# RMSNorm and matmul on one core: loads of x two pairs of tiles earlier, squares up to two pairs earlier, inverse roots in the pair after their roots

## The chip, the core and the metric

The kernel runs on one core of a Trainium2 chip. The core has five engines, each with its own instruction stream: TensorE (matmuls and transposes; PE in the profile, PEld its weight loads), VectorE (DVE), ScalarE (ACT), GpSimd (POOL) and SyncE (SP). An engine works through its stream in order and stops in front of an instruction whose semaphores are not there yet. Transfers between the chip's main memory and the on-chip memory (SBUF) are issued by an engine and then carried out by 16 DMA engines; here SyncE and ScalarE issue them, each on a queue of its own. Matmul results stand in PSUM, from which VectorE or ScalarE copies them.

The metric is the device time of one execution in microseconds; lower is better.

## The reference

Each of the 16 x 1024 rows of `x` (512 numbers, float32) is divided by its root mean square, multiplied by `gamma`, and multiplied by a 512 x 768 matrix.

```python
def reference(x, gamma, weight, eps):
    rms = np.sqrt(np.mean(x ** 2, axis=-1, keepdims=True) + eps)
    x_norm = x / rms * gamma
    return np.matmul(x_norm, weight).astype(np.float32)
```

`x` is 33.6 MB, the output 50.3 MB.

## The kernel before

**Tiles and pairs.** The 16,384 rows make NT = 128 tiles of 128 rows, worked on in NP = 64 pairs; the main loop (L414) runs over pairs j, with tiles 2j and 2j + 1. `gamma` is folded into the weights once at the start (`weights`, L374). The division by the root mean square is done last, on the matmul's result, since it is one number per row.

**One tile's way.** A load brings eight tiles at once into `xt` (two buffers of 16 tiles, so 32 tiles are on chip; L154). GpSimd casts them to bf16 (`cast`, L185, into `xb`; `cast_quad`, L266, into `xq`). TensorE transposes the `xb` tiles into PSUM (`transpose_word`, L235) and VectorE copies them out into `xT` (`evac`, L244). The last four tiles of each 16 ("quads") go another way: VectorE transposes blocks of 32 x 32 from `xq` to `xTq` (`move`, L279, three of sixteen in each pair), and TensorE has no transposes for them. TensorE then makes eight matmuls for each tile into one of three accumulators in PSUM (`matmuls`, L315; `product`, L307). The result is scaled by the inverse root of the row and written to `ot` (`finish_tile`, L326): the even tile of a pair by ScalarE (L288), the odd one by VectorE (L290). `ot` has three buffers of eight tiles; when the eighth is written, SyncE stores the buffer (`store`, L297, issue at L302). A tile can be written into a buffer only after the store of three groups ago has landed.

**The norms.** ScalarE squares each tile with a running sum (`square`, L194: two instructions, L205), which goes to `ssq`. For a group of four pairs it then takes the roots at once (`root`, L208, instruction L210), and VectorE inverts them (L212) into `rstd`, which both scales read. `NORM_GROUPS` (L221) lists the groups: pairs 5 and 6, then 7 to 10, 11 to 14 and so on, and the last five. `norm_turns` (L223) says which pairs are squared in turn j: from j = 7 on pair j + 4. Before that the first pairs are squared one or two at a time.

**Loads.** `load_until` (L181) issues loads in order up to a tile. The first 32 tiles are loaded at the start on SyncE's queue, with the weights; the twelve loads from tile 32 on go on ScalarE's queue (`load`, L174), so each stands in ScalarE's stream among squares and scales. L429 issues the load of tiles 32 to 39 at j = START = 4 and the others at every j > 4 with (j + LEAD) divisible by 4, up to tile 2(j + LEAD) + 8. With LEAD = 14 that is j = 6, 10, 14, ...: tiles 2(j + 14) onwards, fourteen pairs ahead. Such a load overwrites the tiles 32 before, and waits for their squares and casts.

**What sets the order.** The code lists operations in one sequence (`Order`, L21), with what each reads and writes; each engine's stream is its share of the sequence, and `emit` (L39) adds the waits. So the place of a call in the loop is its place in its engine's stream. In turn j come, in this order: casts, moves (L424), norms (L425 to L428), loads (L429), then the pair's matmuls, with the transposes of pair j + 2 between them (`feeder`, L334), and the two scales.

Of the kernel before, what the change touches and what calls it, by code (L numbers as in the profile page):

```python
# [100 lines left out]
def kernel(  # L101
# [12 lines left out]
    def run(engine, issue, reads=(), writes=()):  # L114
        order.add(1, engine, issue, reads, writes)
# [6 lines left out]
    NT = N // P  # L122
    NP = NT // 2
    XG, OG = 16, 8
    FIRST, START, LEAD = 2 * XG, 4, 14

    def stretches(group, parts):
        first, size, i = {}, {}, 0
# [45 lines left out]
    def load(i):  # L174
        dst, to = x_of(i, x_size[i])
        queue = SP if i < FIRST else ACT
        order.transfer(queue, lambda: queue.dma_start(out=dst, in_=rows(x, i, x_size[i])), writes=to)
# [3 lines left out]
    def load_until(i):  # L181
        while starts and starts[0] < i:
            load(starts.pop(0))

    def cast(i, n=1):  # L185
        src, of = x_of(i, n)
        s = i // 8 % 2
        run(POOL, lambda: POOL.tensor_copy(out=xb[s][:, i % 8:i % 8 + n, :], in_=src), of, cells("xb", s, i % 8, n))  # L188
# [5 lines left out]
    def square(i):  # L194
        src, of = x_of(i)
        n = squares[0]
        squares[0] += 1
        if n < 4:
            to, dst = [("jk", n % 2)], jk[n % 2]
        else:  # L200
            n = (n - 4) % SPARE
            to, dst = [("spare", n)], spares[:, n, :]
            if squares[0] <= 4 + SPARE:
                to.append(("w_f", n * K // SPARE))
        run(ACT, lambda: ACT.activation(out=dst, in_=src[:, 0, :], func=AF.Square, accum_out=ssq[:, i:i + 1]),  # L205
            of, to + [("ssq", i)])

    def root(i, n):  # L208
        s = slice(i, i + n)
        run(ACT, lambda: ACT.activation(out=rms[:, s], in_=ssq[:, s], func=AF.Sqrt, scale=1.0 / D, bias=eps_sb),  # L210
            [("ssq", t) for t in range(i, i + n)] + ["eps"], [("rms", i)])
        run(DVE, lambda: DVE.reciprocal(out=rstd[:, s], in_=rms[:, s]), [("rms", i)],  # L212
            [("rstd", t) for t in range(i, i + n)])

    def norms(i, n):
        for t in range(n):
            square(i + t)
        root(i, n)


    NORM_GROUPS = [(5, 2), (7, 4)] + [(f, 4) for f in range(11, NP - 5, 4)] + [(NP - 5, 5)]  # L221
    norm_end = {f + s - 1: (2 * f, 2 * s) for f, s in NORM_GROUPS}
    norm_turns = {3: [5], 4: [6], 5: [7, 8], 6: [9, 10], **{j: [j + 4] for j in range(7, NP - 6)}, NP - 6: [NP - 2, NP - 1]}  # L223

    def norms_of_group(j):
        square(2 * j)
        square(2 * j + 1)
        if j in norm_end:
            root(*norm_end[j])

    def bank(j, t):

        return (j + t) % 2 if j < 3 else j % 2
# [29 lines left out]
    def quad_of(j):  # L263
        return j // 2 if (2 * j) % XG >= XG - 4 and 2 * j >= XG else None

    def cast_quad(q):  # L266
        src, of = x_of(4 * q, 4)
        s = 4 * q // XG % 2
        run(POOL, lambda: POOL.tensor_copy(out=xq[s], in_=src), of, [("xq", s)])  # L269
        for t in range(4):  # L270
            xT_of[4 * q + t] = (xTq[s][:, t], [("xTq", s, n) for n in range((P // B) ** 2)])
        words = xq[s].rearrange("p t d -> p (t d)").bitcast(F32).rearrange("p (a w) -> p a w", w=P)
        turned = xTq[s].rearrange("p t h m c -> p (t h m c)").bitcast(F32).rearrange("p (a m) -> p a m", m=P)
        for tokens in range(0, P, B):
            for features in range(0, P, B):
                quad_moves.append((turned[features:features + B, :, tokens:tokens + B],
                                   words[tokens:tokens + B, :, features:features + B], s, len(quad_moves)))

    def move(dst, src, s, n):  # L279
        run(DVE, lambda: DVE.transpose(out=dst, in_=src), [("xq", s)], [("xTq", s, n)])  # L280

    def move_quad(n):
        for _ in range(min(n, len(quad_moves))):
            move(*quad_moves.pop(0))
# [9 lines left out]
    def accumulator():  # L294
        return next(turns) % 3
# [19 lines left out]
    def matmuls(i, a, ks, feed=None):  # L315
        block, of = xT_of[i]
        for k in ks:
            lhsT = block[:, k // 2, :, k % 2]
            hold(lhsT, of)
            for half, lo, hi in ((0, 0, WIDE), (1, WIDE, O)):  # L320
                product(ops[a][:, lo:hi], lhsT, w_bf[:, k, lo:hi], k == 0, k == K - 1,
                        of + [("w", k, half)], [("ops", a, half)])
            if feed:
                feed()

    def finish_tile(i, a, engine):  # L326
        s = i // OG % 3

        before = [("ot", s, i % OG - 1)] if i == o_first[i] + o_size[i] - 1 else []
        scale(engine, ot[s][:, i % OG, :], ops[a][:, :O], rstd[:, i:i + 1],  # L330
              [("ops", a, 0), ("ops", a, 1), ("rstd", i)] + before, [("ot", s, i % OG)])
        store(i)

    def feeder(pairs, gaps, alone=False):  # L334
        queue = [(j, t, h) for j in pairs for t in range(2) for h in range(2)]
        calls = iter(gaps)

        def feed():
            for _ in range(next(calls)):
                j, t, h = queue.pop(0)  # L340
                transpose_word(j, t, h)
                if alone and h == 1:
                    evac(j, t, 1)
                elif (t, h) == (1, 1):
                    evac(j)
        return feed
# [41 lines left out]
    cast(1)  # L388
    cast(2, 2)
    norms(0, 2)  # L390
    warm_up(2)
    transpose_tile(0)
# [8 lines left out]
    weights(2, DVE)  # L401
    weights(3, ACT)
    norms(2, 2)
    cast(4, 2)
    matmuls(0, acc[0], [2, 3])
# [8 lines left out]
    for j in range(1, NP):  # L414
        if j in (1, 2):
            cast(4 * j + 4, 4)
        elif j % 8 == 4 and j + 4 < NP:
            cast(2 * j + 8, 8)
        elif j % 8 == 6 and j + 2 < NP:
            cast(2 * j + 12, 4)  # L420
        if (2 * j + 2) % XG == 0 and 2 * j + 2 < NT:
            cast_quad((2 * j + 2 + XG - 4) // 4)
        elif 2 * j >= XG:
            move_quad(3)  # L424
        if j < 4:  # L425
            norms(2 * j + 2, 2)
        for pair in norm_turns.get(j, []):
            norms_of_group(pair)  # L428
        if j == START or j > START and (j + LEAD) % 4 == 0:  # L429
            load_until(2 * XG + OG if j == START else 2 * (j + LEAD) + OG)  # L430
        if j < 3:
            feed = feeder([j + 1], mid if j == 1 else one, alone=j == 1)
        elif j == 3:
            feed = feeder([4, 5], both)
        elif j + 2 < NP and quad_of(j + 2) is None:
            feed = feeder([j + 2], two)
        else:
            feed = None
        for i, engine in ((2 * j, ACT), (2 * j + 1, DVE)):
            a = accumulator()  # L440
            matmuls(i, a, range(K), feed)
            finish_tile(i, a, engine)
# [48 lines left out]
```

## Time and profile before

| | |
|---|---|
| time, median of 3 runs | 209.63 us (208.72 to 209.78) |
| the profiled execution | 208.59 us, span 206.6 us |
| mean granted TensorE clock | 0.981 |
| squares, L205 | 124 of 619 ns and 191 ns to `w_f` (as scratch), 4 to `jk` |
| scale on ScalarE, L288 | 64 of 898 ns |
| scale on VectorE, L290 | 64 of 1013 ns |
| root, L210, 128x8 form | 13 of 302 ns |
| inverse root, L212, 128x8 form | 13 of 204 ns |
| load of eight tiles on ScalarE's queue | 12 of 2,048 KB, median 19.5 us from issue to landing |
| store of eight tiles | 13 of 3,072 KB, median 22.6 us from issue to landing |
| HBM read and written | 35.13 MB and 50.33 MB |

The time is that of the whole execution; the span runs from the first to the last instruction that the profiler saw. Busy times of different engines overlap, so they don't add up to the span. "Idle before" an instruction names what ended the engine's wait; it matters only if another engine was waiting in turn. A landing time counts from the issue, so it holds the wait behind earlier transfers of the same queue and beside those of the other.

### The profile page before, as it was taken

To read this page: it belongs to the slowest core of one execution; us is meant where nothing else is said; L and a number is where in the kernel's file an instruction comes from. 1 tells how busy PE (TensorE), PEld (TensorE's weight loads), DVE (VectorE), ACT (ScalarE), POOL (GpSimd) and SP (SyncE) were. 2 spreads that over 40 slices of the span, in tenths; PEclk is the share of its full clock that TensorE was granted. 3 is DMA by queue.
4 is the path that set the end of the run, shared out by engine and by line. 5 is a ranking of instruction groups with operands and counts; after the bars stand their busy time and mean duration, and the time that the engine had idled before them with its cause. 6 is when DMAs were issued, how large, how long until landed. Compare 5 with 4: busy or idle time off the path is not lost.

```text
span 206.6 us, 2755 instructions
## 1 busy us (share of the span) xinstructions
PE 193.4 (94%) x1212; PEld 72.6 (35%) x717; DVE 149.5 (72%) x255; ACT 144.3 (70%) x343; POOL 59.9 (29%) x34
## 2 busy tenths in 40 slices
PE   6699999999999999999999999999999999999940
PEld 0134444433334333433333333433344324343310
DVE  0446556999579975999569974999569974999530
ACT  2698998777777687677877687676948758683310
POOL 1436752067005250063304242060703307000000
PEclk9799999999999999999999999999999999999995
DMA  5999999999999999999999999999999999999993
GB/s 207 428 444 425 412 388 423 423 441 425 433 428 425 428 438 427 424 430 425 431 438 425 425 433 417 443 424 424 428 425 438 433 428 428 436 424 405 416 418 165
DMA packets 5920, 85.62 MB, mean 414 GB/s; under 512 B 658, under 2 KB 660, under 8 KB 1556
## 3 DMA queue, kind: packets, MB, share of 16 engines
q1 hardware_dynamic: 4176, 60.29, 69.0%
q10 hardware_dynamic: 1732, 25.17, 28.7%
q8 instruction: 7, 0.11, 0.2%
q14 instruction: 5, 0.04, 0.0%
HBM read 35.13 MB, written 50.33 MB: 414 GB/s over the span
## 4 chain that ended last, share of the span: by engine, by line
PE 75%; DMA 15%; DVE 5%; issue 1%; ACT 1%; SPq 0%; ACTq 0%
PE ps L309 66%; DMA out_dram<-ot 12%; PE ps L239 9%; DMA xt<-in_x_dram 2%; DVE ot L290 2%; DVE xT L248 1%; DVE xTq L280 1%; ACT ot L288 0%; ACT jk L205 0%; DVE w_bf L290 0%; DVE rstd L212 0%; ACT rms L210 0%; SPq L486 0%; ACTq L93 0%; SPq L445 0%
## 5 line engine op out<-in xcount | busy, mean ns | idle before, releaser
L309 PE MATMUL ps<-w_bf,xT 128*128 128x256 bf16 (+1 forms) x783 | 145.7, 326 | 1.8 <-DVE w_bf L290 0.5
L288 ACT ACTIVATE ot<-ps,rstd 128x768 f32<-128x768 f32 x64 | 57.5, 898 | 47.4 <-PE ps L309 38.0
L188 POOL CAST xb<-xt 128x2048 bf16<-128x2048 f32 (+3 forms) x21 | 46.4, 2218 | 113.3 <-PE ps L239 57.4
L205 ACT ACTIVATE w_f<-xt 128x512 bf16<-128x512 f32 x124 | 76.3, 619 | 0.1
L290 DVE TENSOR_SCALAR ot<-ps,rstd 128x768 f32<-128x768 f32 x64 | 64.8, 1013 | 10.3 <-PE ps L309 9.3
L305 PEld LDWEIGHTS <-xT 128*128 128x128 bf16 x400 | 39.4, 98 | 60.4 <-issue 59.1
L239 PE MATMUL ps<-ident_f,xb 128*128 128x128 f32 x200 | 54.0, 273 | 1.7 <-POOL xb L188 1.6
L248 DVE COPY xT<-ps 128x1024 bf16<-128x1024 bf16 (+1 forms) x53 | 34.6, 654 | 24.3 <-PE ps L239 23.7
L280 DVE STREAM_TRANSPOSE xTq<-xq 32x256 f32<-32x256 f32 x112 | 48.7, 435 | 1.9
L239 PEld LDWEIGHTS ps<-ident_f,xb 128*128 128x128 f32 x200 | 28.1, 141 | 46.6 <-issue 43.8
L309 PE MATMUL ps<-w_bf,xTq 128*128 128x256 bf16 (+1 forms) x217 | 41.8, 324 | 0.4
L205 ACT ACTIVATION_READ_ACCUMULATOR w_f<-xt 128x1 f32 x124 | 23.6, 191 | 0.0
L305 PEld LDWEIGHTS <-xTq 128*128 128x128 bf16 x112 | 11.0, 98 | 14.5 <-issue 14.5
L269 POOL CAST xq<-xt 128x2048 bf16<-128x2048 f32 x7 | 13.3, 1893 | 0.0
L212 DVE RECIPROCAL rstd<-rms 128x8 f32<-128x8 f32 (+3 forms) x20 | 3.9, 193 | 8.9 <-ACT rms L210 8.7
L210 ACT ACTIVATE rms<-ssq,eps_sb 128x8 f32<-128x8 f32 (+3 forms) x20 | 6.0, 300 | 0.7
L309 PE MATMUL ps<-warm 128*128 128x512 bf16 x10 | 4.3, 568 | 1.4 <-DVE eps_sb L363 1.4
L205 ACT ACTIVATE jk<-xt 128x512 bf16<-128x512 f32 x4 | 2.5, 618 | 3.1 <-DMA xt<-in_x_dram 3.1
L288 ACT ACTIVATE w_bf<-w_f,g_sb 128x768 bf16<-128x768 f32 x2 | 1.9, 936 | 1.1 <-DMA w_f<-in_weight_dram 1.1
L386 DVE COPY g_sb<-ps 128x4 f32<-128x4 f32 x1 | 0.2, 161 | 3.1 <-PE ps L380 3.1
L350 ACT ACT_TABLE_LOAD x1 | 1.3, 1283 | 1.5 <-SPq L445 1.5
L290 DVE TENSOR_SCALAR w_bf<-w_f,g_sb 128x512 bf16<-128x512 f32 (+2 forms) x3 | 1.4, 481 | 0.6 <-DMA w_f<-in_weight_dram 0.6
(12 smaller groups left out, 3.0 us busy)
## 6 DMA issues: line engine op xcount, KB each, us to landing
out_dram<-ot SPq DMA_DIRECT2D x13, 3072.0 KB, 22.6
xt<-in_x_dram ACTq DMA_DIRECT2D x12, 2048.0 KB, 19.5
xt<-in_x_dram SPq DMA_DIRECT2D x3, 2048.0 KB, 17.7
out_dram<-ot SPq DMA_DIRECT2D x4, 1536.0 KB, 10.8
out_dram<-ot SPq DMA_DIRECT2D x3, 768.0 KB, 6.7
xt<-in_x_dram SPq DMA_DIRECT2D x2, 1024.0 KB, 6.9
w_f<-in_weight_dram SPq DMA_DIRECT2D x2, 768.0 KB, 7.1
out_dram<-ot SPq DMA_DIRECT2D x2, 384.0 KB, 20.5
```

Source lines behind the costliest of these rows:

```text
L188: run(POOL, lambda: POOL.tensor_copy(out=xb[s][:, i % 8:i % 8 + n, :], in_=src), of, cells("xb", s, i % 8, n))
L205: run(ACT, lambda: ACT.activation(out=dst, in_=src[:, 0, :], func=AF.Square, accum_out=ssq[:, i:i + 1]), of, to + [("ssq", i)])
L210: run(ACT, lambda: ACT.activation(out=rms[:, s], in_=ssq[:, s], func=AF.Sqrt, scale=1.0 / D, bias=eps_sb), [("ssq", t) for t in range(i, i ...
L212: run(DVE, lambda: DVE.reciprocal(out=rstd[:, s], in_=rms[:, s]), [("rms", i)], [("rstd", t) for t in range(i, i + n)])
L239: run(PE, lambda: PE.transpose(out=tp[b][:, t, h, :], in_=words[:, lo:lo + P], identity=ident_f), cells("xb", s, j % 4 * 2 + t) + ["ident" ...
L248: run(DVE, lambda: DVE.tensor_copy(out=dst[:, t:t + n, :], in_=src[:, t:t + n, :]), [("tp", b)], cells("xT", j % 4, t, n))
L269: run(POOL, lambda: POOL.tensor_copy(out=xq[s], in_=src), of, [("xq", s)])
L280: run(DVE, lambda: DVE.transpose(out=dst, in_=src), [("xq", s)], [("xTq", s, n)])
L288: run(ACT, lambda: ACT.mul(out=dst, in_=src, mul=r), reads, writes)
L290: run(DVE, lambda: DVE.tensor_single_scalar(out=dst, in_=src, scalar=r, op=mybir.AluOpType.mult), reads, writes)
L305: run(PE, lambda: PE.ldweights(lhsT), of)
L309: run(PE, lambda: PE.add_instruction(mybir.InstMatmult(name=nc.get_next_instruction_name(), engine=mybir.EngineType.PE, ins=[PE.lower_ap(r ...
```

## The change

Three things move; no operation is added or left out.

- **Loads.** LEAD is 16. Tiles 32 to 39 are still loaded at j = 4 and tiles 40 to 47 at j = 6; from then on loads stand at j = 8, 12, 16, ..., and bring tiles 2(j + 16) onwards. Before they stood at j = 10, 14, 18, ...
- **Squares.** Turns 7 to 14 square pair j + 4 as before; turn 15 squares pairs 19 and 20; turns 16 to 22 pair j + 5; turn 23 pairs 28 and 29; from turn 24 on it is pair j + 6. Roots follow the last square of their group, so from the group of pairs 19 to 22 on they come a turn earlier, and two turns earlier from that of pairs 27 to 30 on.
- **Inverse roots.** The reciprocal is taken out of `root` into `invert`. From j = 8 on a root's reciprocal is issued in the next turn, ahead of the squares and behind VectorE's moves; for j below 8, and for the first pairs (`norms`), it follows its root in the same turn.

```diff
-    FIRST, START, LEAD = 2 * XG, 4, 14
+    FIRST, START, LEAD = 2 * XG, 4, 16
...
             [("ssq", t) for t in range(i, i + n)] + ["eps"], [("rms", i)])
+
+    def invert(i, n):
+        s = slice(i, i + n)
         run(DVE, lambda: DVE.reciprocal(out=rstd[:, s], in_=rms[:, s]), [("rms", i)],
             [("rstd", t) for t in range(i, i + n)])
...
         root(i, n)
+        invert(i, n)
...
-    norm_turns = {3: [5], 4: [6], 5: [7, 8], 6: [9, 10], **{j: [j + 4] for j in range(7, NP - 6)}, NP - 6: [NP - 2, NP - 1]}
+    norm_turns = {3: [5], 4: [6], 5: [7, 8], 6: [9, 10], **{j: [j + 4] for j in range(7, 15)}, 15: [19, 20],
+                  **{j: [j + 5] for j in range(16, 23)}, 23: [28, 29], **{j: [j + 6] for j in range(24, NP - 6)}}
+    inverts = []
...
             root(*norm_end[j])
+            inverts.append(norm_end[j])
...
             move_quad(3)
+        while inverts:
+            invert(*inverts.pop(0))
         if j < 4:
             norms(2 * j + 2, 2)
         for pair in norm_turns.get(j, []):
             norms_of_group(pair)
-        if j == START or j > START and (j + LEAD) % 4 == 0:
-            load_until(2 * XG + OG if j == START else 2 * (j + LEAD) + OG)
+        if j < 8:
+            while inverts:
+                invert(*inverts.pop(0))
+        if j in (START, START + 2) or j > START + 2 and j % 4 == 0:
+            load_until(2 * (j + LEAD) + OG if j > START + 2 else 2 * XG + OG * (j - START + 2) // 2)
```

## The prediction

> **What bounds the kernel now.** First the page's totals, slices and queues, then the chain of waits in order of time, the waits by engine, the timeline of ScalarE around the output buffers, and the DMA queues stretch by stretch.
>
> ```profile
> span 206.6 us, 2755 instructions
> ...
> PE 193.4 (94%) x1212; PEld 72.6 (35%) x717; DVE 149.5 (72%) x255; ACT 144.3 (70%) x343; POOL 59.9 (29%) x34
> ...
> DMA  5999999999999999999999999999999999999993
> GB/s 207 428 444 425 412 388 423 423 441 425 433 428 425 428 438 427 424 430 425 431 438 425 425 433 417 443 424 424 428 425 438 433 428 428 436 424 405 416 418 165
> ...
> q1 hardware_dynamic: 4176, 60.29, 69.0%
> q10 hardware_dynamic: 1732, 25.17, 28.7%
> ```
>
> Two resources are full at once. TensorE is busy for 94%. The 16 DMA engines show a 9 in all slices but the first and last, and the two queues (q1 is SyncE's: first loads, weights, all stores; q10 is ScalarE's: the twelve later loads) fill 69.0 + 28.7 = 97.7% of them. Total bytes don't change, so the DMA engines have next to nothing to give; what can change is whose bytes go first.
>
> ```profile
> 0.94 4.93 DMA xt<-in_x_dram
> ...
> 142.42 25.11 DMA out_dram<-ot
> ...
> 167.62 0.91 ACT ot L288
> ...
> 168.57 1.79 PE ps L309 x10
> ...
> 198.69 1.02 DVE ot L290
> ```
>
> The chain is TensorE nearly throughout, with one detour: a store issued at 142.42 lands 25.11 us later, ScalarE then writes a tile into the freed `ot` buffer, and TensorE waits for that.
>
> ```profile
> ACT ot L288 <- DMA out_dram<-ot: 9.2, 4, 2.7
> DVE rstd L212 <- ACT rms L210: 8.7, 10, 2.9
> PE ps L309 <- ACT ot L288: 0.4, 1, 0.4
> ```
>
> ```profile
> 131.22 0.90 ACT L288 ACTIVATE ot<-ps,rstd 128x768 f32<-128x768 f32 x1 [1.90 <-DMA out_dram<-ot]
> ...
> 143.34 0.90 ACT L288 ACTIVATE ot<-ps,rstd 128x768 f32<-128x768 f32 x1 [1.88 <-DMA out_dram<-ot]
> ...
> 155.48 0.90 ACT L288 ACTIVATE ot<-ps,rstd 128x768 f32<-128x768 f32 x1 [2.74 <-DMA out_dram<-ot]
> ...
> 167.62 0.90 ACT L288 ACTIVATE ot<-ps,rstd 128x768 f32<-128x768 f32 x1 [2.73 <-DMA out_dram<-ot]
> ```
>
> ScalarE waits four times (tiles 80, 88, 96, 104), because the buffer's store of three groups ago lands too late; only the last wait gets through to TensorE, by 0.42 us. The three accumulators in PSUM hide the others. How near they are: tile 102's scale starts at 162.77 on TensorE's release. A pair takes 3.03 us with transposes (59.98 to 63.01 between two scales) and 2.60 without (192.19 to 194.79), so tile 104 is ready at 162.77 + 1.52 + 1.30 = 165.59. Tile 107 needs its accumulator 2.60 later, and the scale takes 0.95 with its semaphores: 1.65 us of tolerance. The landing left tile 104 waiting 167.62 - 165.59 = 2.03; 0.38 too much, near the 0.42 seen. Tile 96 was ready at 150.62 + 2 x 1.52 = 153.66 (tile 94's scale: 150.62), waited 1.82, and with transposes behind it tolerates 3.04 - 0.95 = 2.09. **0.27 us are left there.** So stores that land later stop TensorE almost at once.
>
> **The change part by part.** No instruction is added or removed; the sum is over places. It is made against the profiled 208.59 us (span 206.6 and 2.0 around it), which is 1.04 below the median 209.63 of the three runs; the difference is carried over.
>
> *Reciprocals* (L212, 13 in the 128x8 form of 0.20 us). VectorE's 8.7 us behind the roots shrink, 3.8 of them in that form. TensorE waited for VectorE's copies only early on (1.2 us on the weight loads), so the gain is 0. A new wait: at j = 11 the reciprocal now stands behind the scale of tile 21 and three moves (45.62 + 1.33), so it ends at about 47.0, while tile 22's scale on ScalarE started at 45.67. It holds up two squares and that accumulator, which tile 25 needs at 45.67 + 1.52 + 1.30 = 48.5; released at 47.0 + 0.9 = 47.9, 0.6 us to spare. At j = 15 it ends at 55.70 + 1.01 + 0.2 = 56.9, when tile 30's scale starts (56.94). Later groups have their root a pair sooner. Cost 0; up to 1.3 without that cover.
>
> *Squares.* Turns 15 and 23 carry four squares instead of two. Two follow each other in the ScalarE timeline at 0.61 us, so +1.22 us against 0.92 of idle before tile 30's scale: 0.3 late, inside the tolerance of 1.65 or more. They also read x sooner: tiles 104 on behind tile 90's scale (ends 145.37 + 0.89 = 146.26) and tiles 120 on behind tile 106's (170.53), while GpSimd's casts show these loads landed at 145.89 and 170.51. Cost 0 if loads land no later than now; 0 to spare at the last one.
>
> *Loads.* The first two on ScalarE's queue stay (j = 4 and 6). Load 48 goes from j = 10 (41.75) to j = 8, behind tile 14's scale and two squares, about 36.1. All later ones move by two pairs, some 3.6 to 6 us. Their destinations were cast long before (48 overwrites tiles 16 to 23, cast by 28), so no new wait stands ahead of the issues. What does it give the loads? The queues by stretch (36 to 42, 42 to 48, 47 to 57 us):
>
> ```profile
> q10 hardware_dynamic: 93, 1.51, 59.6%
> ...
> DMA packets 175, 2.65 MB, mean 442 GB/s; under 512 B 31, under 2 KB 31, under 8 KB 31
> ...
> q10 hardware_dynamic: 53, 0.62, 24.3%
> ...
> q1 hardware_dynamic: 115, 2.46, 57.8%
> q10 hardware_dynamic: 114, 1.79, 41.9%
> ```
>
> From 42 to 48 the load queue ran dry (between 43 and 45 it moved 0.00 MB): load 40 was done, load 48 just issued. Before that it had 59.6%, against stores of short rows; from 47 on 41.9%, its steady share beside 24 KB rows (60 to 168: 40.1%). With load 48 issued at 36 the hole closes. At 59.6% throughout it gains 0.596 x 2.65 - 0.62 = 0.96 MB; at 41.9% 0.49; at 0% of the hole, if an earlier issue brings no earlier data, 0. Half of each gives 0.72; the change from one load to the next costs it too (57 to 59: 32.8%, or 0.08 MB less). I take **0.64 MB**, and 0 and 0.96 as the ends.
>
> After that both queues always have work and share as now, 60 to 40, which is also their demand (3,072 KB of stores to 2,048 KB of loads for eight tiles). So loads stay 0.64 MB ahead (3.7 us at 175 GB/s) and stores 0.64 MB behind: 0.64 / 0.253 = 2.5 us later (59% of 429 GB/s, from 60 to 63 us), until the loads end near 167 instead of 170. Nothing in TensorE's path wants x sooner: its waits for casts end before 9 us.
>
> *Where the 2.5 us go.* Tile 96 had 0.27 to spare: TensorE stops for 2.23 us there or, partly, already at tiles 80 and 88. Tile 104 then comes 2.2 later itself and needs no more. TensorE ends 2.23 - 0.42 = 1.81 us later, the last store is issued at 200.00 + 1.81.
>
> *The end.* That store took 5.66 us to land (5.7 is the least of all stores), since others were ahead of it on full engines. A store of 768 KB alone is priced by the first load: 4.93 us for 1,024 KB, of which 1.05 MB / 427 GB/s = 2.46 move data and 2.47 are fixed; 0.79 MB then make 1.84 + 2.47 = 4.32. So 1.34 us of the queueing can swallow delay: the work that the stalled TensorE did not deliver, the DMA engines use to catch up. 1.81 - 1.34 = **+0.47 us**: 208.59 + 0.47 + 1.04 = **210.1**.
>
> By the Trainium skill ("DMA: Bandwidth & Descriptors", Anatomy of one DMA) a DMA takes about 2.0 us and its bytes at 436 GB/s, fitted on GpSimd's path: 3.8 us for this store, by which the end would move by an estimated 0; the 4.93 us of the first load here stand above that fit (4.4), so the row's price is kept.
>
> **The rivals.** *Nothing moves* (17%): the hole at 42 to 48 closes later or the loads gain nothing. For it: 57 to 59 us shows a dip although load 56 had been issued at 53.24. Against: that dip is 32.8%, the hole 0. Stores land as before, 209.6.
>
> *The loads take all of it* (17%), the slower side: TensorE at the `ot` buffers becomes the bound. Place: tiles 80 to 104. At 0.96 MB the stores come 3.8 us late, the stop is 3.5, the net 3.1, the end +1.8: **211.4**. It decides by more than 0.5% from a net of 1.34 + 1.05 = 2.39 us on, that is stores 3.1 us late or 0.78 MB. For it: while short store rows lasted the loads had 59.6%, and delayed short rows last longer. Against: store 24.54 with the short rows had landed at 45.3.
>
> *Squares wait for x* (5%): if loads land 3 us later than now, ScalarE stands in front of tile 108's scale; 3 less the tolerance 1.65 is 1.35 more on TensorE, on top of the forecast: 211.4. Against: longer queues serve loads sooner, not later.
>
> *Faster* (15%): the DMA engines lose less. The slices from 36 us on below 420 (417, 405, 416, 418) lack 12 + 24 + 13 + 11 = 60 GB/s to 429, x 5.165 us = 0.31 MB or 0.7 us; with the 0.42 us stop gone as well, -1.1: **208.5**. For it: engines without a dry queue and stores alone after 167 us. Against: the last three of these slices lie where TensorE delivers, not where loads run.
>
> The Trainium skill (same page, Where 436 GB/s comes from) puts the ceiling of the 16 engines at 435 GB/s; 60 to 168 us ran at 429, so by it an estimated 1.4%, or 2.8 us of all 85.62 MB, is the most that any order could bring.
>
> **How the numbers follow.** 0.5%, about what a measurement of this kernel can tell from no change, is 1.05 us. Forecast 46%, 210.1: of it 36 within, 10 slower (stop longer by 0.6). Nothing moves: 15 within, 2 faster. All of it: 15 slower, 2 within. Squares: 4 slower, 1 within. Faster: 13 faster, 2 within. Together 15 faster, 56 within, 29 slower. Range: 208.5 less 0.2 to 211.4 plus 0.5 (half the spread of the three runs). The forecast alone: 209.4 to 210.8.
>
> **What would show it.** Right: the queue at 42 to 48 us without the hole (load share 40% or more), last load landed near 167 to 168, ScalarE's waits for stores starting at tile 72 or 80 and summing to well over 9.2 us, TensorE's waits for ScalarE near 2 us instead of 0.4, the last scale near 200.5 instead of 198.69, last store landing in some 4.5 us instead of 5.66, VectorE's wait for roots under 6. Wrong: store landings as before, waits of ScalarE on x, or TensorE ending by 199.

## The result, and the profile after

The changed kernel takes 210.94 us (median of 20 runs, 208.75 to 213.28), the kernel before 209.07 (median of 20 runs beside them, 208.55 to 211.79). The ratio is 1.0060, with a 95% interval of 1.0032 to 1.0089: slower by 1.3 us, 0.7 to 1.9. The ratio leaves out the executions more than 1.5% above the fastest of their kernel, which the medians hold. The profiled execution of the changed kernel is one of its quicker ones, 209.56 us.

Its page, with the slices and the queues:

```profile
span 207.6 us, 2771 instructions
...
DMA  5999999999999999999999999999999999999887
GB/s 204 425 433 452 382 411 415 436 430 429 428 437 420 436 425 426 420 429 429 429 429 415 418 428 423 420 436 417 425 426 420 431 440 422 406 417 414 367 353 296
...
q1 hardware_dynamic: 4176, 60.29, 69.2%
q10 hardware_dynamic: 1732, 25.17, 28.5%
```

The queues move the same packets and bytes as before. New is the end: before, the three slices ahead of the last had 405, 416 and 418 GB/s; now they have 414, 367 and 353, and more is left for the last (296 instead of 165). The DMA engines no longer have a stock of finished tiles to write, because these come too late.

The waits by engine (engine, line, waited for; total us, times, longest):

```profile
DVE rstd L215 <- ACT rms L210: 6.2, 4, 2.9
...
ACT ot L295 <- DMA out_dram<-ot: 23.6, 10, 2.7
...
PE ps L316 <- ACT ot L295: 1.8, 4, 0.5
```

ScalarE's waits for a free `ot` buffer have gone from 4 to 10 and from 9.2 to 23.6 us. Before, they began at tile 80; ScalarE's timeline shows the first one now at tile 32, and there is one in every group of eight tiles from there to tile 104:

```profile
47.83 0.90 ACT L295 ACTIVATE ot<-ps,rstd 128x768 f32<-128x768 f32 x1 [2.49 <-PE ps L316]
...
62.34 0.90 ACT L295 ACTIVATE ot<-ps,rstd 128x768 f32<-128x768 f32 x1 [2.49 <-DMA out_dram<-ot]
...
74.48 0.90 ACT L295 ACTIVATE ot<-ps,rstd 128x768 f32<-128x768 f32 x1 [2.68 <-DMA out_dram<-ot]
```

(The first line is tile 22, which comes up below.) The waits for stores are 12.1 us apart, the pace at which groups are stored. VectorE's timeline shows what that does to the pace of the tiles, here the scales of tiles 63 and 79, first in the kernel before:

```profile
105.58 1.01 DVE L290 TENSOR_SCALAR ot<-ps,rstd 128x768 f32<-128x768 f32 x1
...
129.00 1.01 DVE L290 TENSOR_SCALAR ot<-ps,rstd 128x768 f32<-128x768 f32 x1
```

and in the changed kernel:

```profile
107.55 1.01 DVE L297 TENSOR_SCALAR ot<-ps,rstd 128x768 f32<-128x768 f32 x1
...
131.80 1.01 DVE L297 TENSOR_SCALAR ot<-ps,rstd 128x768 f32<-128x768 f32 x1
```

Sixteen tiles took 23.42 us before and take 24.25 now. Sixteen tiles are 10.49 MB of loads and stores, and 10.49 MB in 24.25 us are 432 GB/s, about what the DMA engines of the kernel before moved when both queues were full (429 GB/s from 60 to 168 us). From about tile 40 to tile 103 the kernel goes at the pace of the DMA engines, and TensorE falls back by 0.83 us in every sixteen tiles. Its last tile is scaled at 201.94 instead of 198.69. Of these 3.25 us, 0.58 belong to this execution: tile 0 was scaled at 12.61 instead of 12.03, ahead of every instruction that moved.

Why the stores land later, by the DMA queues from 28 to 48 us (packets, MB, share), first in the kernel before:

```profile
q10 hardware_dynamic: 308, 4.52, 53.8%
q1 hardware_dynamic: 446, 4.05, 47.9%
```

and in the changed kernel:

```profile
q10 hardware_dynamic: 339, 5.03, 59.1%
q1 hardware_dynamic: 426, 3.64, 43.2%
```

The load queue (q10) moved 0.51 MB more, the store queue (q1) 0.41 MB less. From 42 to 48 us alone the load queue now has this, where it had 24.3% before:

```profile
q10 hardware_dynamic: 88, 1.18, 46.0%
```

The stretch in which it had run empty is gone.

That is not all. Each transfer is split over the 16 DMA engines and is done when the last of them is. The trace holds the 16 completions of each transfer. For the store of tiles 8 to 15, and later for all kernels, in us from its issue:

```
                 first   median   last engine   last minus first
before            18.6     19.4      21.4          2.9
changed           18.4     20.0      25.3          6.9
loads_only        18.9     19.4      23.8          4.9
norms_only        19.2     19.9      21.6          2.4
gap_kept          16.5     18.0      21.3          4.7
one_early         18.2     19.6      21.7          3.6
one_queue_16      14.9     15.3      17.9          2.9
one_queue_14      15.3     16.0      18.0          2.7
wide_first_16     18.1     18.4      20.2          2.1
wide_first_14     19.1     19.8      20.9          1.9
mid_first_16      21.1     22.5      24.7          3.7
narrow_first_16   24.0     24.9      26.5          2.5
narrow_first_14   18.2     19.4      21.7          3.4
```

In the changed kernel the middle engine finishes 0.6 us later than before, the last one 3.9. Stores stay 6.6 to 6.9 us apart between first and last engine until 159 us. Loads are as far apart or further, with one engine ahead: on load 48 it finishes 3.1 us before the next. That fits one engine that had served the loads first and was behind with the stores; the completions don't name their engine, so this is inferred.

The kernel before had had such a lag too. Its third store (tiles 2 and 3) ended 5.8 us apart, at 41.0 us; the fourth (tiles 4 to 7), which ran through the empty stretch of the load queue, ended 1.4 us apart, at 45.3. In the changed kernel, without that stretch, the same two stores ended 7.2 and 6.9 us apart.

At the end, the stretches 192 to 201 and 201 to 207 us (busy time and count of PE, PEld, DVE, ACT, POOL; clock; DMA share; GB/s), before:

```profile
192.00:201.00 9.00, 6.60 (x41) 1.86 (x19) 3.71 (x5) 2.70 (x3) 0.00 (x0) 1.00 0.98 414
201.00:207.00 6.00, 0.00 (x0) 0.00 (x0) 0.00 (x0) 0.00 (x0) 0.00 (x0) 0.59 0.41 172
```

and after:

```profile
192.00:201.00 9.00, 9.00 (x58) 2.66 (x28) 5.85 (x9) 3.06 (x4) 0.00 (x0) 1.00 0.85 355
201.00:207.00 6.00, 0.90 (x6) 0.18 (x2) 1.02 (x1) 0.54 (x1) 0.00 (x0) 0.98 0.84 346
```

Before, the DMA engines were full to 201 us and only had the rest to do. Now they stand idle for 15% of the nine microseconds in which TensorE still works, and make up for it when it has finished. The bound of the last stretch has gone from the DMA engines to TensorE.

### The profile page after: what moved, and what is told of

It is laid out like the page before. It is cut to its first block, busy times and chain, and to the rows that moved or that the text cites. A ratio compares the mean times of both kernels' runs of the same rounds, so it can differ in the third digit from the quotient of the medians.

```text
span 207.6 us, 2771 instructions
## 1 busy us (share of the span) xinstructions
PE 196.5 (95%) x1236; PEld 72.7 (35%) x717; DVE 149.4 (72%) x255; ACT 143.1 (69%) x343; POOL 60.0 (29%) x34
## 4 chain that ended last, share of the span: by engine, by line
PE 45%; DMA 39%; DVE 10%; ACT 2%; issue 1%; ACTq 0%; SPq 0%; DVEq 0%
PE ps L316 40%; DMA out_dram<-ot 37%; PE ps L246 5%; DVE ot L297 4%; DVE xTq L287 3%; DMA xt<-in_x_dram 2%; DVE xT L255 2%; ACT ot L295 1%; ACT jk L205 0%; DVE rstd L215 0%; DVE w_bf L297 0%; ACT rms L210 0%; ACTq L93 0%; DVEq L93 0%; SPq L498 0%
## 5 line engine op out<-in xcount | busy, mean ns | idle before, releaser
L316 PE MATMUL ps<-w_bf,xT 128*128 128x512 bf16 (+1 forms) x800 | 150.2, 328 | 2.8 <-ACT ot L295 1.8
L316 PE MATMUL ps<-w_bf,xTq 128*128 128x512 bf16 x224 | 42.8, 326 | 0.0
```

The lines of the kernel that those rows point to most:

```text
L316: run(PE, lambda: PE.add_instruction(mybir.InstMatmult(name=nc.get_next_instruction_name(), engine=mybir.EngineType.PE, ins=[PE.lower_ap(r ...
```

## The experiments

Theory A: without the empty stretch the 16 engines stay out of step between the two queues, and a store waits for the slowest. Theory B, the forecast's: all engines give the loads a larger share. Theory C: squares and reciprocals cost. Theory D: a longer load queue delays the stores all along. Runs beside those of the kernel before; ratios are to it.

**Loads alone**, LEAD 16 in the kernel before:

```diff
-    FIRST, START, LEAD = 2 * XG, 4, 14
+    FIRST, START, LEAD = 2 * XG, 4, 16
...
-        if j == START or j > START and (j + LEAD) % 4 == 0:
-            load_until(2 * XG + OG if j == START else 2 * (j + LEAD) + OG)
+        if j in (START, START + 2) or j > START + 2 and j % 4 == 0:
+            load_until(2 * (j + LEAD) + OG if j > START + 2 else 2 * XG + OG * (j - START + 2) // 2)
```

> Loads sixteen pairs ahead; squares four ahead and reciprocals behind their roots as before. Theory A (closing the load queue's empty stretch at 43 to 45 us keeps the 16 DMA engines out of step between their two queues, so that a store lands when its slowest engine is done, some 4 us later): like the changed kernel, 0.4 to 1.0% above before, ScalarE waits for stores in 8 or more places, the last store landing of one group 6 us or so behind its first engine. Theory B (all engines give the loads 0.64 MB more, as forecast): also 0.2 to 0.8% above before, but the engines stay within 3 us of each other. Theory C (the squares and reciprocals cost): within 0.2% of before.

Ratio 1.0082 (1.0039 to 1.0126). The waits by engine:

```profile
ACT ot L288 <- DMA out_dram<-ot: 21.8, 8, 3.6
...
PE ps L309 <- ACT ot L288: 3.7, 6, 1.1
```

The loads alone carry the cost. The table shows something more: the middle engine finishes the store as early as before (19.4 us), and only the last is late (23.8). Here nearly all of the lateness is the engines' being apart, as A has it; the spread was 4.9 us instead of the 6 that A named, and 7.5 by the store that landed at 160 us.

**Squares and reciprocals alone**, the changed kernel with the loads of before:

```diff
-    FIRST, START, LEAD = 2 * XG, 4, 16
+    FIRST, START, LEAD = 2 * XG, 4, 14
...
-        if j in (START, START + 2) or j > START + 2 and j % 4 == 0:
-            load_until(2 * (j + LEAD) + OG if j > START + 2 else 2 * XG + OG * (j - START + 2) // 2)
+        if j == START or j > START and (j + LEAD) % 4 == 0:
+            load_until(2 * XG + OG if j == START else 2 * (j + LEAD) + OG)
```

> Squares up to six pairs ahead and reciprocals a pair behind their roots; loads as before. Theories A and B: within 0.3% of before, four or five waits of ScalarE for stores. Theory C: 0.4 to 1.0% above before.

Ratio 1.0029 (1.0000 to 1.0058), four waits of ScalarE for stores, 8.2 us. Not C's size, but a small cost isn't excluded by this run; wide_first_16 below, with both parts and no loss, speaks against it.

**The empty stretch kept**, load 48 back at j = 10 in the changed kernel:

```diff
-        if j in (START, START + 2) or j > START + 2 and j % 4 == 0:
-            load_until(2 * (j + LEAD) + OG if j > START + 2 else 2 * XG + OG * (j - START + 2) // 2)
+        if j in (START, START + 2, START + 6) or j > START + 4 and j % 4 == 0 and j > 8:
+            load_until(2 * (j + LEAD) + OG if j % 4 == 0 and j > START else {4: 40, 6: 48, 10: 56}[j])
```

> The changed kernel, but the load of tiles 48 to 55 goes back from turn 8 to turn 10, so the load queue runs empty around 44 us again; the ten later loads stay two pairs earlier. Theories A and B: within 0.3% of before, stores landing as before, four or five waits of ScalarE. Theory D (the longer load queue delays the stores all along): like the changed kernel, 0.4 to 1.0% above before.

Ratio 1.0017 (0.9996 to 1.0038). One load two turns later takes most of the loss away by the middle values (the two intervals still overlap, from 1.0032 to 1.0038), though ten others are as early as in the changed kernel. ScalarE waits for stores five times, as A and B had it, and D's 0.4% or more falls. The load queue's share from 42 to 48 us was 29.4%. The engines still came only partly together (4.7 us apart at this store, 5.1 to 5.8 later), and the profiled execution was the slowest of its twelve runs.

**One early load**, load 48 alone from j = 10 to j = 8 in the kernel before:

```diff
-        if j == START or j > START and (j + LEAD) % 4 == 0:
-            load_until(2 * XG + OG if j == START else 2 * (j + LEAD) + OG)
+        if j == START or j > START and (j + LEAD) % 4 == 0 or j == 8:
+            load_until(2 * XG + OG if j == START else 56 if j == 8 else 2 * (j + LEAD) + OG)
```

> The kernel before, with the load of tiles 48 to 55 alone moved from turn 10 to turn 8. Theories A and B: 0.4 to 1.0% above before; the store of tiles 8 to 15 lands at 61 us or later instead of 57.8, and under A its last engine 5 us or more behind its first. Theory D: within 0.3% of before.

A miss for A and B: ratio 1.0009 (0.9975 to 1.0042), the store landed at 58.6. From 52 to 58 us the queues show why:

```profile
q1 hardware_dynamic: 90, 1.84, 74.1%
q10 hardware_dynamic: 57, 0.74, 28.8%
```

The empty stretch was not closed but put off: load 56, still at its old place, is issued at 53.7, one engine has been done with load 48 since 50.9, and others follow from 54.8 on. On load 48 the engines ended 8.7 us apart, on load 56 2.7. That fits an empty queue letting the engines fall into step again, at 44 us or later. It is D's number, but gap_kept speaks against D: as far as these intervals tell, it takes the early load 48 and early loads behind it to lose time. The times scatter widely, though: five of the twelve were 208.6 to 209.0 us, seven 209.7 to 212.6.

**One queue**, all loads on SyncE, in the changed kernel and in the one before:

```diff
-        queue = SP if i < FIRST else ACT
+        queue = SP
```

> The changed kernel with all loads on SyncE's queue, so loads and stores go through the DMA engines in one order, a store and a load in turn. Theory A (engines out of step between two queues): engines within 1 us of each other at every landing, the store of tiles 8 to 15 lands by 59 us, few waits of ScalarE for stores before 130 us, time 0 to 0.8% below the kernel before and 0.6% or more below the changed one. Theory B (loads take the stores' share, no matter on which queue): stores as late as in the changed kernel, time 0.4 to 1.0% above before.

> The kernel before with all loads on SyncE's queue. The order of transfers on that queue is the same as in one_queue_16, only the issues of the loads come two pairs later; the queue always has work. A and B: within 0.3% of one_queue_16, since an earlier issue then changes no order on the DMA engines. If the early loads cost by something else than the two queues' sharing (their places on ScalarE, their destinations), one_queue_16 is 0.4% or more slower than this.

Ratios 1.0001 (0.9977 to 1.0025) and 1.0002 (0.9981 to 1.0024). The two halves don't differ in when loads are issued, though: in both, SyncE issues each later load 0.4 us behind the same store, load 48 at 37.1 and 36.4 us, load 56 at 50.1 and 48.7. So the pair says nothing on two pairs sooner within one queue; its halves differ in the squares and reciprocals alone, which cost nothing here. The comparison with the kernels of two queues says more. Loads 48 and 56 were issued at 41.75 and 53.24 in the kernel before and at 34.3 and 48.0 in the changed one. So both halves have them 3 to 5 us sooner than the kernel before and within 3 us of the changed one, and neither is shown to be slower than the kernel before. In one queue stores and loads land in the order of their issue (in one_queue_16 store 8 to 15 at 54.6, load 48 at 59.5, the next store at 66.8, load 56 at 71.6). So B, in the form that early loads cost on any queue, falls: the cost is in the sharing between two queues. The store of tiles 8 to 15 lands within 17.9 us of its issue (A had asked for landing by 59 us: 54.6), and ScalarE waits for no store in the first, for one in the second. Wrong was that engines would stay within 1 us (2.9 and 2.7), and that the time would fall much.

**The first stores**, 4 + 4 tiles instead of 1 + 1 + 2 + 4, in both kernels:

```diff
-    o_first, o_size = stretches(OG, {0: [1, 1, 2, 4], last - 1: [4, 4], last: [4, 2, 2]})
+    o_first, o_size = stretches(OG, {0: [4, 4], last - 1: [4, 4], last: [4, 2, 2]})
```

> The changed kernel with the first eight tiles stored as 4 + 4 instead of 1 + 1 + 2 + 4, so no rows of 3 and 6 KB stand against the loads' 16 KB rows at 27 to 42 us. Theory A with the small rows as the cause of the engines' lag: engines within 4 us of each other from 60 us on, stores 2 us or more sooner than in the changed kernel, time within 0.3% of before. If the lag has another cause: spread of 6 us or more stays, 0.4 to 1.0% above before.

> The kernel before with the first eight tiles stored as 4 + 4. Control for wide_first_16: all theories within 0.3% of before.

Ratios 0.9986 (0.9965 to 1.0008) and 0.9998 (0.9978 to 1.0018). With the loads at the changed kernel's places, its loss is gone; all twelve runs lie between 208.7 and 209.4 us. The load queue didn't run empty here (its share was 40.3% from 42 to 48 us), but the store of tiles 4 to 7 already ended only 2.1 us apart, so that there was little for an empty stretch to mend. Its queues from 28 to 48 us and its waits:

```profile
q10 hardware_dynamic: 301, 4.41, 51.5%
q1 hardware_dynamic: 318, 4.28, 50.2%
```

```profile
ACT w_f L205 <- DMA xt<-in_x_dram: 3.9, 3, 1.7
ACT ot L295 <- DMA out_dram<-ot: 2.8, 2, 1.5
```

The store queue has 318 packets to move there instead of 426 for more bytes (4.28 MB instead of 3.64), and the engines stay 2.1 us apart. ScalarE even waits 3.9 us for x in its early squares, at no cost.

**More and fewer short rows.** The same list as 2 + 2 + 4 in the changed kernel, and as eight single tiles in both:

```diff
-    o_first, o_size = stretches(OG, {0: [1, 1, 2, 4], last - 1: [4, 4], last: [4, 2, 2]})
+    o_first, o_size = stretches(OG, {0: [2, 2, 4], last - 1: [4, 4], last: [4, 2, 2]})
...
+    o_first, o_size = stretches(OG, {0: [1] * 8, last - 1: [4, 4], last: [4, 2, 2]})
```

> The changed kernel with the first eight tiles stored as 2 + 2 + 4: rows of 6 and 12 KB, three quarters as many store rows as in 1 + 1 + 2 + 4. Theory A+B (on each DMA engine the two queues take turns row by row, so each short store row costs a 16 KB row's time beside loads, and without an empty stretch of the load queue the engines stay apart): between wide_first_16 and the changed kernel, 0 to 0.4% above before, engines 2 to 5 us apart at the store landings. If only the 3 KB rows did harm: like wide_first_16.

> The changed kernel with the first eight tiles stored one by one: twice as many short store rows. Theory A+B: worse than the changed kernel, 0.8 to 2.5% above before, stores 5 us or more later than in the kernel before, ScalarE waiting for stores from tile 24 or 32 on. If the rows of the first stores don't matter (only the order of issues): as the changed kernel.

> The kernel before with the first eight tiles stored one by one. Theory A+B: the load queue runs empty earlier and longer and lets the stores catch up, so 0.1 to 0.8% above before, clearly less than narrow_first_16. If short rows cost by themselves: as much above before as narrow_first_16 is above the changed kernel.

2 + 2 + 4: ratio 1.0005 (0.9980 to 1.0031); the profiled execution, the slowest of its runs (210.84 us), shows the whole trouble (nine waits, 23.5 us); the other ten took 208.7 to 210.1 us. The time fits both expectations. Eight singles with early loads: 1.0068 (1.0037 to 1.0098), below the expected 0.8% with its middle and not by its interval; not shown to be worse than the changed kernel. ScalarE's waits for stores began at tile 32, as foretold. With the loads of before: 1.0007 (0.9992 to 1.0022). That is just under the foretold range: short rows alone cost nothing that can be measured; short rows with early loads do. From 28 to 48 us in narrow_first_16:

```profile
q10 hardware_dynamic: 431, 6.28, 73.3%
q1 hardware_dynamic: 813, 2.24, 27.9%
```

The loads have taken 73%. The engines are only 2.5 us apart at the store of tiles 8 to 15, and yet it lands 26.5 us after its issue, since all engines are late alike (median 24.9). So B's way of being late, by share, and A's, by engines apart, each make the kernel slower; by this store, loads_only is nearly pure A, narrow_first_16 nearly pure B, and the changed kernel 0.6 us of B and 3.3 of A in its profiled execution. The share and the spread were not set apart within one and the same kernel.

No version is shown to beat the kernel before: wide_first_16 comes nearest, and its interval holds 1.

## Why the prediction was right, and where it was off

*The sign and the place* were right. The load queue's empty stretch at 42 to 48 us closed, the loads took the stores' share, stores landed later, ScalarE waited for `ot` buffers and TensorE behind it (1.8 us in four places, foretold near 2). loads_only, gap_kept, the one-queue runs and wide_first_16 together show that this is the cause. The extra bytes were put at 0.64 MB; 0.51 were measured. Load 48 went sooner than foretold, at 34.30 us and not at about 36.1.

The size was not right. Slower by more than 0.5% was given 29%, and the 0.6% measured lies there; the measured +1.3 us is nearer to the +1.8 of *the loads take all of it* than to the forecast's +0.47. The 210.1 also stands on a base that came out 0.56 us too high (209.63 from three runs, 209.07 from twenty), which brought it nearer to the 210.94.

*The reciprocals* at no cost: right. The reciprocal that tile 22 needs ended at 47.73 in VectorE's timeline, and the tile's scale started at 47.83, after 2.49 us of idle (0.92 in the kernel before). The profile names TensorE as the one waited for, but TensorE had released this scale at 45.67 in the kernel before, which is 46.25 here. Less the 0.58 of this execution the scale's start is 47.25, foretold "about 47.0". TensorE didn't stop there. VectorE's waits for roots fell from 8.7 to 6.2 us, not quite under 6. *The squares* at no cost: right; no wait of ScalarE for x appears in the changed kernel's profile beyond the 3.1 us at the start that the kernel before has too.

*The step that failed* is the term "2.5 us later" for the stores. It took the 16 engines for one. The middle engine was 0.6 us late, the slowest, which decides, 3.9. With it went the place: instead of one stop of 2.23 us near tile 96 the kernel went at the pace of the DMA engines for some sixty tiles, at 0.83 us for each sixteen. ScalarE's waits began at tile 32, not at 72 or 80, and here the forecast didn't follow its own term: before, tile 32's scale started at 59.98, only 2.20 us after the store that it needs had landed (57.78), so 2.5 us would have been enough. "Tile 104 needs no more" held: TensorE's last stop of these is at 148 us, behind tile 88. TensorE's net delay was 3.25 - 0.58 = 2.67 us instead of 1.81.

*The end* was mis-sized the other way. The last store was priced at 4.32 us from a load's 4.93; it took 3.40, as the least of the landing times shows:

```profile
DMA to landing us min/median/max: 3.4/24.1/26.5
```

So 5.66 - 3.40 = 2.26 us of delay could be swallowed, not 1.34. In the profiled execution 2.67 - 2.26 = 0.41 us were left, beside the +0.47 forecast: two errors that cancel, so the agreement is luck. Span 207.6 - 206.6 = 1.0 is these 0.41 and the late start of 0.58. The 20 runs give 1.3 us (0.7 to 1.9), so the typical loss was larger than the forecast; how much later TensorE ended in the slower ones can't be seen without their profiles. That the 16 engines fall apart more in some runs than in others would fit the wide spread of the runs (one_early, mid_first_16), but each kernel has one profile, so this stays open.

*The last load* was to land near 167 to 168 us; it landed at 170.26. Its middle engine had it at 167.7. *Nothing moves*, *squares wait* and *faster* didn't happen; *the loads take all of it* is what narrow_first_16 made by force.

## What to carry to other kernels

When the DMA engines are full, issuing loads earlier brings no data for free: it takes turns from the stores, and whoever waits for buffers pays. While both have work, two queues share the DMA engines row by row, so a queue of short rows loses to one of long rows; look at the rows' sizes where both are busy, and put transfers whose order matters on one queue. A queue that runs empty for a moment can be useful where the engines have fallen out of step, and a landing time is that of the slowest of 16 engines, which a median or a mean over the queue hides.

## What the runs showed of the hardware

- While both have work, the two queues take turns by packets, whatever their size. From 48 to 60 us in the kernel before, with rows of 24 KB and 16 KB:

```profile
q1 hardware_dynamic: 141, 3.07, 60.0%
q10 hardware_dynamic: 141, 2.05, 40.1%
```

  The Trainium skill ("DMA: Bandwidth & Descriptors", Queues, rings and completion order) says that each engine goes round the queues that have work, packet by packet; the equal counts agree. With store rows of 3 KB beside loads of 16 KB, in narrow_first_16 from 36 to 44 us, it was 193 packets to 196, and 0.51 MB to 2.95.
- Engines that had fallen out of step between two queues stayed so in the changed kernel, where neither queue ran empty: 6.9 us between first and last on the store that landed at 62 us, 6.7 on the one at 159 us. The Trainium skill (same page, Why a DMA increments its semaphore by 16 and not by 1) has the 16 engines finish independently and the semaphore count them all, which the landing times bear out.
- A store of 768 KB with little ahead of it landed in 3.40 us, where a load of 1,024 KB at the start took 4.93: less the bytes at 427 GB/s (the rate of the kernel before from 47 to 57 us), that is 1.56 us and 2.47.
- All loads and stores in one queue keep the DMA engines as full as two: 97.4% in one_queue_16, 69.0 + 28.7 = 97.7% before.
